# Attention operands of 128 rows in a hybrid decoder trunk: scores from stacked high and low parts, meta values in four groups, a new head order

## The chip, the cores and the metric

The kernel runs on one core of a Trainium2 chip. The metric is the device time of one execution in microseconds (us); of several runs the median is given. One execution was profiled, and all rows below come from it.

## What is computed

The trunk has two layers. The first mixes with a gated linear recurrence, the second with differential attention; a gated MLP with a short causal convolution follows each. 16 learned meta tokens stand ahead of the 512 tokens, so T = 528, D = 1024, 8 heads, and each head has two maps (m = 0, 1) of 64 dimensions. The part that matters here:

```python
def diff_attention(x, w_qkv, lq1, lk1, lq2, lk2, subln_g, w_o, lambda_init):
    q, k, v = jnp.split(x @ w_qkv, 3, axis=-1)     # per head: q, k (2, T, 64), v (T, 128)
    q = apply_rope(q, cos, sin) * (d ** -0.5)
    k = apply_rope(k, cos, sin)
    def attend(q_blk, q_pos):
        s = jnp.einsum('bhmqd,bhmkd->bhmqk', q_blk, k)
        s = jnp.where(mask, s, -jnp.inf)
        p = jax.nn.softmax(s, axis=-1)
        wgt = p[:, :, 0] - lam * p[:, :, 1]
        return jnp.einsum('bhqk,bhkv->bhqv', wgt, v)
    ...                                             # the 16 meta queries, then 4 blocks of 128
    o = rmsnorm(o, subln_g) * (1.0 - lambda_init)
    return o @ w_o
```

## The kernel before

Activations lie with the model dimension on the 128 partitions and tokens along the row. A float32 operand x is used as two rounded parts, hi (a copy of x) and lo = x - hi, so that a product is three matmuls of the fast type: hi hi, lo hi, hi lo (`block_mm`, lines 584 to 595). Weights come as a stream of 128 x 1024 units: SyncE loads a unit (`raw`), ScalarE makes `whi`, VectorE `wlo` (lines 478 to 491). `next_block` asks for units up to seven ahead (line 529).

Nothing is issued in the order of the code. Every operation is a step with an estimated cost for the engines it may run on, and `Program.order` (lines 267 to 348) makes one static order for each engine: it always takes the step that can start first by its estimates, the older one of two, within a window of 180 steps. Buffers of the tag "t" (53 of them) and "half" (5), and the 8 accumulator banks, are given out in that order as well. A step with two possible engines (a copy out of the accumulators) goes to the one that is free first.

In the attention stage `attn_order` (line 96) gives the sequence of the big steps: q, k, v project one head; S makes its scores, A its output, M the meta queries of four heads, W the first half of one tile of the output product. Their steps are interleaved by the planner.

- `rope` (line 1020) projects q or k, rotates it on VectorE (`ra`, `rb`), splits it into a high part (`x[0]`, ScalarE) and `low` (VectorE), and lets SyncE move halves of 64 partitions (`move`, line 1017). Map 0 lies on partitions 0 to 63, map 1 on 64 to 127. For q, `x[m]` gets high and low of map m, one above the other; for k, `x[m]` gets the high part of map m twice, and `low` stays as it is.
- `scores(hd, i)` (line 1061), for query tile i of 128 queries and N = 16 + 128 (i + 1) keys: `score` (line 1069) makes two matmuls for each map. The first is of 128 rows (`k,q` in the rows), the second is of 64 rows, the high q with the low k (`low,q`). For i up to 2 both maps lie in one pair of banks and the order is first, first, second, second; for i = 3 each map has two halves of 264 keys and first and second alternate. Then mask and maximum (VectorE), `e` = exponential (ScalarE), the weights `e` (VectorE: reciprocal, `f`, sum of both maps), transposes of the weights into `tr`, and copies to `wt` (128 real keys a block) and `wm` (the 16 meta keys).
- `values` (line 1050) transposes v in the same way; the 16 meta rows go to `vm`.
- `attend` (line 1108), for each i: one product of the meta keys, 16 rows (`vm,wm`), and i + 1 products of 128 rows (`v,wt`). These are plain float32, and each is two passes (two rows of the profile).
- `meta_queries` (line 1132) does all this for 4 x 4 meta queries at once.

Of the kernel before, what the change touches and what calls it, by code (L numbers as in the profile page):

```python
# [12 lines left out]
F32 = mybir.dt.float32  # L13
# [5 lines left out]
P = 128  # L19
D = 1024  # L20
KD = D // P
SEQ = 512
NMETA = 16
T = SEQ + NMETA
TH = T // 2
OFF1 = 12
# [28 lines left out]
TAIL_TILES = 2  # L55
TBUFS = 53
SBUFS = 30
AHEAD = 180

SPARE = 2  # L60
# [35 lines left out]
def attn_order():  # L96


    order = "q0 k0 q1 S0 k1 v0 q2 A0 k2 S1 k3 k5 v1 q3 S2 k4 S3 v2 q4 A1 v4 A2 v3 S4 k6 A3 q5 q6 A4 S5 k7 v5 S6 q7 v6 S7 A6 M0 v7 W0 A5 W1 W2 W3 W4 W5 M1 W6 A7 W7"
    return [(x[0], int(x[1:])) for x in order.split()]  # L100


# [102 lines left out]
class Program:  # L205
# [61 lines left out]
    def order(self):  # L267
# [9 lines left out]
        while len(out) < len(self.steps):  # L277
# [4 lines left out]
            for e, now in free.items():  # L282
                first = None
                for s in open_steps[e]:
                    if s.rank > oldest + AHEAD:
                        continue
                    start = max(now, s.ready)
                    for b in s.bufs:
                        if b.tag is None or b in held:
                            continue  # L290
                        if b.tag in BANKS:
                            at = self.find_banks(BANKS[b.tag], 0 if s.rank == oldest else s.spare)
                            start = max(start, at[0]) if at else math.inf
                            if not at:
                                break
                            continue
                        if not slots[b.tag]:
                            start = math.inf
                            break
                        start = max(start, slots[b.tag][0])  # L300
                    key = (start, s.rank)
                    if start < math.inf and (first is None or key < first[0]):
                        first = (key, start, s, e)
                if first and (best is None or first[0] < best[0]):
                    best = first
# [53 lines left out]
def trunk_kernel(ctx: ExitStack, tc: tile.TileContext, xT, wstream, wup, par, cst, out):  # L359
# [16 lines left out]
    }  # L376

    def place(tag, bufs):
        places[tag] = lambda b: wp.tile(b.shape, b.dtype, name=b.name, tag=tag, bufs=bufs)

    for tag, n_bufs in w_slots.items():
        place(tag, n_bufs)
# [621 lines left out]
    meta = t_tile("meta", F32, HEADS // MGROUP * GQ + HEADS * NMETA)  # L1004
    qms = [meta[:, g * GQ:(g + 1) * GQ] for g in range(HEADS // MGROUP)]
    km = meta[:, HEADS // MGROUP * GQ:]
    vm = [t_tile(f"vm{i}", F32, 4 * P) for i in range(2)]
    fill(meta, 0.0)
    swap = [(i + 16) % 32 for i in range(32)]
    qk, v_of, sums, wts, wms, o_n = {}, {}, {}, {}, {}, {}  # L1010

    def vmeta(hd):
        return vm[hd // 4].part(hd)[:NMETA, (hd % 4) * P:(hd % 4 + 1) * P]

    ROWS = [slice(64 * m, 64 * m + 64) for m in range(2)]

# [3 lines left out]
    def rope(kind, hd):  # L1020
        segs, n, hn, c0 = (TAIL, T1, TH1, OFF1) if kind == "q" else (FULL, T, TH, 0)
        acc = project(norm.xs, segs, kind)
        a, b = t_tile("ra", F32, n), t_tile("rb", F32, n)
        vec("stream_shuffle", h2(b, 0, hn), acc, swap)
        vec("tensor_tensor", h2(a, 0, hn), acc, h2(cos, c0, hn), op=ALU.mult)
        vec("tensor_tensor", b, b, sin[:, c0:], op=ALU.mult)
        vec("tensor_tensor", a, a, b, op=ALU.add)

        x = [t_tile(f"{kind}{m}", F32R, n) for m in range(2)]
        low = t_tile("low", F32R, n)  # L1030
        top, bottom = ROWS
        act(x[0], a, AF.Copy, n=n)
        vec("tensor_tensor", low, a, x[0].bitcast(F32), n=n, op=ALU.subtract)
        move(x[1].part(1)[bottom], x[0].part(1)[bottom])
        if kind == "q":
            move(x[0].part(1)[bottom], low[top])
            move(x[1].part(0)[top], low[bottom])
        else:
            move(x[1].part(0)[top], x[0].part(1)[bottom])
            move(x[0].part(1)[bottom], x[0].part(0)[top])  # L1040
        qk[kind, hd] = (*x, low)
        if kind == "q":
            for m in range(2):
                g, i = divmod(hd, MGROUP)
                r, col = slice(64 * m, 64 * m + 64), i * 2 * MR + m * MR + i * NQ1
                copy(qms[g].part(("q", hd, m))[r, col:col + NQ1], a[r, :NQ1], n=NQ1, where=("pool",))
        else:
            copy(km.part(("k", hd))[:, hd * NMETA:(hd + 1) * NMETA], a[:, :NMETA], n=NMETA, where=("pool",))

    def values(hd):  # L1050
# [2 lines left out]
        scaled(h2(vt), acc, h2(norm.rstd))  # L1053
        v, tr, trm = t_tile("v", F32, 512), one_tile("tr"), one_tile("tr")
        turn([tr[:, i * P:(i + 1) * P] for i in range(NQT)], [vt[:, NMETA + i * P:NMETA + (i + 1) * P] for i in range(NQT)], ident)
        turn([trm[:NMETA, :P]], [vt[:, :NMETA]], ident)
        copy(v, tr, n=512)
        copy(vmeta(hd), trm[:NMETA, :P], n=P)
        v_of[hd] = v

    def scores(hd, i):
# [5 lines left out]
        S = []  # L1067

        def score(m, o, c0, n):
            return [(o, q[m][:, qs], k[m][:, c0:c0 + n], True, False), (o, q[m].part(m)[ROWS[m], qs], k[2].part(m)[ROWS[m], c0:c0 + n], False, True)]  # L1070

        cost = mm_cost(N)
        if N <= 512:
            s = acc_tile("s")
            (b0, l0), (b1, l1) = (score(m, s[:, m, :N], 0, N) for m in range(2))
            products([b0, b1, l0, l1], 4 * cost, S_SPARE)
            d = s[:, :, N - P:N]
            vec("tensor_tensor", d, d, mask.unsqueeze(1).to_broadcast([P, 2, P]), n=2 * P, op=ALU.add)
            vec("tensor_reduce", mx, s[:, :, :N], n=2 * N, axis=AX.X, op=ALU.max, negate=True)
# [15 lines left out]
        w = es[0]  # L1095
        vec("scalar_tensor_tensor", w, es[1], f, w, n=N, op0=ALU.mult, op1=ALU.add)
        tr, n = one_tile("tr"), (i + 1) * P
        trm = tr[:NMETA, 512 - P:] if n < 512 else one_tile("tr")[:NMETA, :P]
        turn([tr[:, j * P:(j + 1) * P] for j in range(i + 1)], [w[:, NMETA + j * P:NMETA + (j + 1) * P] for j in range(i + 1)], ident)
        turn([trm], [w[:, :NMETA]], ident)  # L1100
        if i == 0:
            wms[hd] = t_tile("wm", F32, 512)
        wt = t_tile("wt", F32, n)
        copy(wt, tr[:, :n], n=n)
        copy(wms[hd].part(i)[:NMETA, i * P:(i + 1) * P], trm, n=P)
        wts[hd, i], sums[hd, i] = wt, rc

    def attend(hd):
# [2 lines left out]
        cols = [slice(i * P, (i + 1) * P) for i in range(NQT)]  # L1111
        for i, c in enumerate(cols):
            oi = o.part(i)[:, c]
            list_ = [(oi, wms[hd].part(i)[:NMETA, c], vmeta(hd), True, False)]
            list_ += [(oi, wts[hd, i][:, cols[j]], v[:, cols[j]], False, j == i) for j in range(i + 1)]
            products(list_, 0.217 * (i + 2), O_SPARE)
        for i, c in enumerate(cols):
            act(junk.part(i)[:, c], o[:, c], AF.Square, n=P, scale=sums[hd, i][:, 0:1], accum_out=ss.part(i)[:, i:i + 1])
        rsqrt_mean(ss, ss, P, NQT)
# [12 lines left out]
    def meta_queries(g):  # L1132
# [10 lines left out]
        act(e, sv, AF.Exp, n=NMETA, bias=mx, accum_out=sm)  # L1143
        vec("reciprocal", sm, sm, n=1)
        vec("tensor_scalar", e, e, sm, coef[:2 * MR], n=NMETA, op0=ALU.mult, op1=ALU.mult)
        tr, w = one_tile("tr"), t_tile("wm", F32, 2 * MR)[:NMETA]
        turn([tr[:NMETA, :2 * MR]], [e], ident[:2 * MR, :2 * MR])
        copy(w, tr[:NMETA, :2 * MR], n=2 * MR, where=("act",))
        vec("tensor_tensor", w[:, :MR], w[:, :MR], w[:, MR:], n=MR, op=ALU.add)
        cols = [slice(i * NQ1, (i + 1) * NQ1) for i in range(MGROUP)]  # L1150
        om_, tot = one_tile("om"), one_tile("tot")
        products([(om_[:, c], vmeta(hd), w[:, c], True, True) for hd, c in zip(hds, cols)], 0.11 * MGROUP)
        om, sq, ro = (t_tile(nm, F32, MR) for nm in ("om", "sq", "ro"))
        copy(om, om_[:, :MR], n=MR, where=("act",))
        act(sq, om, AF.Square, n=MR)
# [156 lines left out]
```

## Time and profile before

| what | value |
|---|---|
| median of 3 runs (lowest to highest) | 1250.38 us (1248.98 to 1251.09) |
| profiled execution, its own time | 1247.84 us |
| its span, first to last instruction | 1245.6 us |
| TensorE busy, share of span | 98% |
| VectorE, ScalarE, GpSimd busy | 79%, 57%, 14% |
| granted clock of TensorE, mean | 0.997 |

PE is TensorE's matmul side, PEld its weight load, DVE is VectorE, ACT ScalarE, POOL GpSimd and SPq SyncE's queue. A matmul's row tells its rows and weight columns, then what is streamed: "64*128 64x264" has 64 rows. Rows of matmuls that follow each other overlap, since they are pipelined; the distance of their starts tells what one costs. The recurrent stage comes first, then the first MLP up to about 570 us, the attention at 575 to 850, and the second MLP behind it.

### The profile page before, as it was taken

The numbers are of one execution on the slowest core, as the hardware profiler recorded it, in microseconds if no ns is written. First come the engines' busy times: TensorE is split into PE (matmuls) and PEld (weight loads), VectorE is DVE, ScalarE is ACT, GpSimd is POOL, SyncE is SP. The second block draws the span as 40 slices with busy tenths as digits, with TensorE's granted clock in tenths as the row PEclk, the third lists the DMA queues.
The fourth block names the chain that finished last, engine by engine and source line by source line (L and its number), as shares of the span: only waits on it lengthen the run. The fifth ranks groups of instructions, "written<-read, shape, count | busy, mean of one in ns | idle before, by whom it ended". The sixth has DMA issues, their size and how long they took to land.

```text
span 1245.6 us, 23369 instructions
## 1 busy us (share of the span) xinstructions
PE 1222.8 (98%) x9288; PEld 1167.6 (94%) x9288; DVE 985.8 (79%) x1562; ACT 714.8 (57%) x1257; POOL 168.4 (14%) x283
## 2 busy tenths in 40 slices
PE   8999999999999999999999999999999999999996
PEld 7999999999999999999988888899999999999985
DVE  6987989977697689779787676668997777778875
ACT  7799565755465466544444444445665555556533
POOL 4000002322222221000000010000222222222100
PEclk9999999999999999999999999999999999999998
DMA  8323425887777877322331233112598777777502
GB/s 302 103 73 102 128 77 128 202 196 184 181 185 175 190 180 195 110 96 73 107 104 54 67 94 136 51 62 91 122 219 202 187 186 186 187 186 183 140 1 68
DMA packets 66350, 171.62 MB, mean 138 GB/s; under 512 B 7872, under 2 KB 10176, under 8 KB 66240
## 3 DMA queue, kind: packets, MB, share of 16 engines
q1 hardware_dynamic: 43200, 128.16, 31.7%
q0 software_dynamic: 23040, 41.95, 20.3%
q8 instruction: 73, 1.20, 0.4%
q14 instruction: 37, 0.30, 0.1%
HBM read 119.63 MB, written 2.10 MB: 98 GB/s over the span
## 4 chain that ended last, share of the span: by engine, by line
PE 82%; DVE 6%; ACT 5%; DMA 3%; issue 2%; POOL 1%; SPq 0%; DVEq 0%; POOLq 0%; ACTq 0%
PE banks L592 45%; PE banks L870 30%; PE banks L463 6%; PE banks L455 2%; ACT L1256 2%; DVE wlo L416 1%; DVE tn L416 1%; ACT r L423 1%; DMA G<-V 1%; ACT whi L485 1%; DVE rc L416 1%; DMA raw<-wstream 1%; ACT tn L423 1%; DMA pt<-par 1%; DMA N<-G 0%
## 5 line engine op out<-in xcount | busy, mean ns | idle before, releaser
L870 PE MATMUL banks<-xh,whi 128*128 128x264 f32 (+1 forms) x960 | 273.3, 285 | 2.3 <-ACT p L431 1.4
L870 PE MATMUL banks<-xl,whi 128*128 128x264 f32 (+1 forms) x960 | 272.6, 284 | 0.0
L870 PE MATMUL banks<-xh,wlo 128*128 128x264 f32 (+1 forms) x960 | 272.1, 283 | 0.0
L592 PE MATMUL banks<-xh,whi 128*128 128x264 f32 (+1 forms) x896 | 188.3, 291 | 8.8 <-ACT whi L423 5.9
L416 DVE TENSOR_TENSOR wlo<-raw,whi 128x1024 fp32r<-128x1024 f32 (+1 forms) x123 | 148.8, 1210 | 59.4 <-ACT whi L485 58.5
L485 ACT CAST whi<-raw 128x1024 fp32r<-128x1024 f32 x121 | 126.2, 1045 | 113.7 <-PE banks L592 46.0
L870 PEld LDWEIGHTS banks<-xh,whi 128*128 128x128 f32 x960 | 181.1, 189 | 6.6 <-ACT p L431 1.9
L870 PEld LDWEIGHTS banks<-xl,whi 128*128 128x128 f32 x960 | 181.2, 189 | 2.2
L592 PE MATMUL banks<-xl,whi 128*128 128x264 f32 (+1 forms) x896 | 182.2, 285 | 0.2 <-DVE xl L416 0.2
L592 PE MATMUL banks<-xh,wlo 128*128 128x264 f32 (+1 forms) x896 | 182.2, 285 | 0.0
L870 PEld LDWEIGHTS banks<-xh,wlo 128*128 128x128 f32 x960 | 181.3, 189 | 0.0
L592 PE MATMUL banks<-actl,whi 128*128 128x264 f32 (+2 forms) x582 | 155.0, 320 | 0.0
L592 PE MATMUL banks<-acth,whi 128*128 128x264 f32 (+2 forms) x582 | 154.9, 320 | 0.0
L592 PE MATMUL banks<-acth,wlo 128*128 128x264 f32 (+2 forms) x582 | 154.6, 319 | 0.0
L592 PEld LDWEIGHTS banks<-xh,whi 128*128 128x128 f32 x896 | 139.1, 190 | 12.3 <-ACT whi L423 5.9
L592 PEld LDWEIGHTS banks<-xl,whi 128*128 128x128 f32 x896 | 139.4, 189 | 0.4 <-DVE xl L416 0.4
L592 PEld LDWEIGHTS banks<-xh,wlo 128*128 128x128 f32 x896 | 139.4, 189 | 0.0
L416 DVE TENSOR_TENSOR h<-banks,h 128x528 f32<-128x528 f32 (+3 forms) x154 | 105.4, 687 | 35.4 <-PE banks L592 34.2
L416 DVE TENSOR_TENSOR wlo<-G,whi 128x512 fp32r<-128x512 f32 (+1 forms) x120 | 103.2, 864 | 23.9 <-ACT whi L577 22.1
L592 PEld LDWEIGHTS banks<-acth,wlo 128*128 128x128 f32 x582 | 96.7, 188 | 8.2
L592 PEld LDWEIGHTS banks<-acth,whi 128*128 128x128 f32 x582 | 96.8, 188 | 6.2
L592 PEld LDWEIGHTS banks<-actl,whi 128*128 128x128 f32 x582 | 96.7, 188 | 6.0
(209 smaller groups left out, 2295.3 us busy)
## 6 DMA issues: line engine op xcount, KB each, us to landing
raw<-wstream SPq DMA_DIRECT2D x105, 512.0 KB, 4.2
G<-wup SPq DMA_DIRECT2D x40, 512.0 KB, 4.0
V<-wup SPq DMA_DIRECT2D x40, 512.0 KB, 3.5
N<-wup SPq DMA_DIRECT2D x40, 256.0 KB, 3.3
G<-V POOLq DMA_DIRECT2D x40, 256.0 KB, 3.6
N<-G POOLq DMA_DIRECT2D x40, 256.0 KB, 4.0
V<-V POOLq DMA_DIRECT2D x40, 256.0 KB, 4.8
G<-N POOLq DMA_DIRECT2D x40, 256.0 KB, 4.4
```

The lines of the kernel that those rows point to most:

```text
L416: step({e: costs[e] for e in where}, lambda e, os_, a, k: getattr(apis[e], fn)(os_[0], *a, **k), [o], args, kw)
L423: nc.scalar.activation(os_[0], a[0], func, **k, **({} if accum_out is None else {"accum_out": os_[1]}))
L455: nc.tensor.transpose(ap(oi), ap(xi), ap(eye))
L463: nc.tensor.matmul(ap(o), ap(l), ap(r), start=start, stop=stop)
L485: prog.add({"act": (n + 118) / 1200}, lambda e: nc.scalar.copy(ap(hi), ap(raw)), [raw], [hi, turn_])
L592: nc.tensor.matmul(a[:, dst, :n], w, m[:, c0:c0 + n], start=s0, stop=s1)
L870: nc.tensor.matmul(a, w[:, c], x, start=start and begin, stop=end, skip_group_check=not start)
L1256: nc.scalar.preload_act_table_set(table)
```

## The change

- k is laid out as high over low (two tiles, no `low` kept), q as high twice and low twice (four tiles). The scores of a map are two matmuls of 128 rows, which give all four products of the parts. First and second of one map stand together. q needs six moves in place of three.
- The 16 meta keys become 64 rows: `meta_parts` writes the high part twice and the low part twice (for v in turns), so that 64 rows of weights times 64 rows of values give all four products. `vm` and `wm` are of the split type, with 64 more rows of zeros that `fill` (GpSimd) writes; the product is one matmul of 128 rows. Each use of `meta_parts` adds a ScalarE copy and a VectorE subtraction of 32 columns ahead of the transpose.
- The meta queries' products of both maps accumulate in the bank, where before the two were added on VectorE.
- `attn_order` has a new sequence; the planner's estimate for `attend` changes. `T_SPARE` is 0, so the changed test for buffers does what it did; the "half" buffers get one common size.

```diff
-    order = "q0 k0 q1 S0 k1 v0 q2 A0 k2 S1 k3 k5 v1 q3 S2 k4 S3 v2 q4 A1 v4 A2 v3 S4 k6 A3 q5 q6 A4 S5 k7 v5 S6 q7 v6 S7 A6 M0 v7 W0 A5 W1 W2 W3 W4 W5 M1 W6 A7 W7"
+    order = "q0 k0 q1 S0 v0 q2 k1 A0 k5 k2 S1 k3 k4 q4 v1 S2 q3 S3 v2 A1 v4 A2 v3 S4 A3 q5 A4 S5 v5 k6 q6 S6 q7 v6 k7 M0 v7 W0 A5 S7 W1 A6 W2 W3 W4 W5 M1 W6 A7 W7"
...
-    vm = [t_tile(f"vm{i}", F32, 4 * P) for i in range(2)]
+    vm = [t_tile(f"vm{i}", F32R, 4 * P) for i in range(2)]
+    for x in vm:
+        fill(x[MSEG:].bitcast(F32), 0.0)
...
+    def meta_parts(name, x, rows=P, turns_=False):
+        o = Buf("half", [rows, MSEG], F32R, name)
+        o4 = o.rearrange("p (a b c) -> p a b c", a=2, b=2)
+        hi, lo = (o4[:, :, i] if turns_ else o4[:, i] for i in range(2))
+        x = x.unsqueeze(1).to_broadcast([rows, 2, NMETA])
+        act(hi, x, AF.Copy, n=2 * NMETA)
+        vec("tensor_tensor", lo, x, hi.bitcast(F32), n=2 * NMETA, op=ALU.subtract)
+        return o.bitcast(F32)
...
-        if kind == "q":
+        if kind == "k":
             move(x[0].part(1)[bottom], low[top])
             move(x[1].part(0)[top], low[bottom])
+            qk[kind, hd] = x
         else:
-            move(x[1].part(0)[top], x[0].part(1)[bottom])
-            move(x[0].part(1)[bottom], x[0].part(0)[top])
-        qk[kind, hd] = (*x, low)
+            low1 = t_tile("low", F32R, n)
+            move(low1.part(1)[bottom], low.part(1)[bottom])
+            for y0, y1 in (x, (low, low1)):
+                move(y1.part(0)[top], y0.part(1)[bottom])
+                move(y0.part(1)[bottom], y0.part(0)[top])
+            qk[kind, hd] = (*x, low, low1)
...
-        turn([trm[:NMETA, :P]], [vt[:, :NMETA]], ident)
+        turn([trm[:MSEG, :P]], [meta_parts("vs", vt[:, :NMETA], turns_=True)], ident)
...
-            return [(o, q[m][:, qs], k[m][:, c0:c0 + n], True, False), (o, q[m].part(m)[ROWS[m], qs], k[2].part(m)[ROWS[m], c0:c0 + n], False, True)]
+            return [(o, q[i][:, qs], k[m][:, c0:c0 + n], i < 2, i >= 2) for i in (m, 2 + m)]
...
-            (b0, l0), (b1, l1) = (score(m, s[:, m, :N], 0, N) for m in range(2))
-            products([b0, b1, l0, l1], 4 * cost, S_SPARE)
+            products(score(0, s[:, 0, :N], 0, N) + score(1, s[:, 1, :N], 0, N), 4 * cost, S_SPARE)
...
-        turn([trm], [w[:, :NMETA]], ident)
+        turn([trm], [meta_parts("ws", w[:, :NMETA])], ident)
...
-            list_ = [(oi, wms[hd].part(i)[:NMETA, c], vmeta(hd), True, False)]
+            list_ = [(oi, wms[hd].part(i)[:, c], vmeta(hd), True, False)]
...
-            products(list_, 0.217 * (i + 2), O_SPARE)
+            products(list_, 0.12 + 0.22 * (i + 1), O_SPARE)
...
-        products([(om_[:, c], vmeta(hd), w[:, c], True, True) for hd, c in zip(hds, cols)], 0.11 * MGROUP)
+        products([(om_[:, c], vmeta(hd), w[:, m * MR + c.start:m * MR + c.stop], m == 0, m == 1) for hd, c in zip(hds, cols) for m in range(2)], 0.22 * MGROUP)
```

How this moves instructions is shown at three places. In these lists `ident` is the unit matrix of a transpose, `e` the weights of a query tile, `ws` the four groups of its meta keys; numbers behind a name tell tiles apart.

TensorE, head 0, the scores of i = 2 and the first product of `attend` behind them. Before:

```order
L455 MATMUL banks<-ident,e 128x128
L455 MATMUL banks<-ident,e 16x128
L592 MATMUL banks<-xh,whi 128x258 x2
L592 MATMUL banks<-xl,whi 128x258 x2
L592 MATMUL banks<-xh,wlo 128x258 x2
L463 MATMUL banks<-k_7139,q_7107 128x400
L463 MATMUL banks<-k_7149,q_7119 128x400
L463 MATMUL banks<-low,q_7107 128x400
L463 MATMUL banks<-low,q_7119 128x400
L463 MATMUL banks<-vm_7325,wm 128x128
L463 MATMUL banks<-v,wt 128x128
```

Now:

```order
L458 MATMUL banks<-ident,ws 64x128
L595 MATMUL banks<-xh,whi 128x264 x2
L595 MATMUL banks<-xl,whi 128x264 x2
L595 MATMUL banks<-xh,wlo 128x264 x2
L466 MATMUL banks<-k_7146,q_7111 128x400
L466 MATMUL banks<-k_7146,low 128x400
L466 MATMUL banks<-k_7156,q_7123 128x400
L466 MATMUL banks<-k_7156,low 128x400
L466 MATMUL banks<-vm_6438,wm 128x128
L466 MATMUL banks<-v,wt 128x128
```

First and second product of a map now follow each other, `low` is q's and not k's, and the transpose of the meta part no longer stands straight behind that of the real keys: here projection blocks lie between them.

VectorE, head 0, around the weights `e` of i = 0. Before:

```order
L416 RECIPROCAL rc<-sm 128x2
L416 TENSOR_TENSOR banks<-banks,mask 128x2x128
L416 SCALAR_TENSOR_TENSOR f<-rc,sm,nlam 128x1
L431 COPY vm_7325<-banks 16x128
L416 TENSOR_REDUCE mx<-banks 128x2
L416 SCALAR_TENSOR_TENSOR e<-e,f 128x144
L416 RECIPROCAL rc<-sm 128x2
L431 COPY wm<-banks 16x128
```

Now:

```order
L419 RECIPROCAL rc<-sm 128x2
L419 TENSOR_TENSOR banks<-banks,mask 128x2x128
L419 SCALAR_TENSOR_TENSOR f<-rc,sm,nlam 128x1
L419 TENSOR_TENSOR ra<-ra,rb 128x516
L419 SCALAR_TENSOR_TENSOR e<-e,f 128x144
L419 TENSOR_REDUCE mx<-banks 128x2
L419 TENSOR_TENSOR low<-ra,q_7343 128x516
L419 TENSOR_TENSOR ws<-e,ws 128x32
```

The subtraction for `ws` is new; here it stands two instructions behind `e`.

SyncE, from the end of a run of weight loads to the moves of head 0's q and k. Before:

```order
L480 DMA raw<-wstream 128x1024 x16
L446 DMA q_7119<-q_7107 64x516
L446 DMA q_7119<-low 64x516
L446 DMA k_7149<-k_7139 64x528 x2
L446 DMA q_7107<-low 64x516
```

Now:

```order
L483 DMA raw<-wstream 128x1024 x15
L449 DMA q_7123<-q_7111 64x516 x2
L449 DMA low<-low 64x516 x2
L449 DMA k_7156<-k_7146 64x528
L449 DMA q_7111<-q_7111 64x516
L449 DMA k_7156<-low 64x528
L449 DMA low<-low 64x516
L483 DMA raw<-wstream 128x1024
L449 DMA k_7146<-low 64x528
```

q's moves are six in place of three, and a weight load now stands among them.

## Rows read from the trace of the kernel before

**Rows 1.** The page, its first part: busy us, share of the span, instructions.

```profile
PE 1222.8 (98%) x9288; PEld 1167.6 (94%) x9288; DVE 985.8 (79%) x1562; ACT 714.8 (57%) x1257; POOL 168.4 (14%) x283
```

**Rows 2.** Busy time by stretch: length, each engine's us, granted clock, DMA share, GB/s.

```profile
580.00:770.00 190.00, 190.00 (x1407) 171.10 (x1405) 148.30 (x315) 87.51 (x240) 7.94 (x23) 1.00 0.32 93
50.00:250.00 200.00, 197.85 (x1601) 195.53 (x1600) 174.49 (x244) 151.19 (x212) 18.80 (x42) 1.00 0.44 118
200.00:250.00 50.00, 48.76 (x388) 47.48 (x388) 47.39 (x74) 34.45 (x61) 15.37 (x25) 1.00 0.82 181
```

**Rows 3.** Groups by shape, 570 to 852 us: count, busy us, mean ns, idle before.

```profile
L463 PE MATMUL banks<-vm,wm 16*128 16x128 f32 x64 | 15.5, 321 | 0.0
...
L463 PE MATMUL banks<-low,q 64*128 64x264 f32 x32 | 12.3, 385 | 0.0
```

**Rows 4.** Timeline of TensorE, a last-tile score: start us, us, what.

```profile
688.93 0.37 PE L463 MATMUL banks<-k,q 128*128 128x264 f32 x1
689.23 0.39 PE L463 MATMUL banks<-low,q 64*128 64x264 f32 x1
689.54 0.39 PE L463 MATMUL banks<-k,q 128*128 128x264 f32 x1
689.86 0.39 PE L463 MATMUL banks<-low,q 64*128 64x264 f32 x1
690.18 0.51 PE L592 MATMUL banks<-xh,whi 128*128 128x264 f32 x2
690.52 0.41 PE L592 MATMUL banks<-xl,whi 128*128 128x264 f32 x2
690.77 0.41 PE L592 MATMUL banks<-xh,wlo 128*128 128x264 f32 x2
```

**Rows 5.** Timeline of TensorE, a score of the first tile.

```profile
699.84 0.34 PE L463 MATMUL banks<-k,q 128*128 128x144 f32 x2
700.11 0.34 PE L463 MATMUL banks<-low,q 64*128 64x144 f32 x2
700.38 0.51 PE L592 MATMUL banks<-xh,whi 128*128 128x264 f32 x2
700.73 0.41 PE L592 MATMUL banks<-xl,whi 128*128 128x264 f32 x2
```

**Rows 6.** Timeline of TensorE, a part of `attend` and the score behind it.

```profile
706.04 0.48 PE L463 MATMUL banks<-vm,wm 16*128 16x128 f32 x2
706.45 0.71 PE L463 MATMUL banks<-v,wt 128*128 128x128 f32 x4
707.10 0.48 PE L463 MATMUL banks<-vm,wm 16*128 16x128 f32 x2
707.51 0.94 PE L463 MATMUL banks<-v,wt 128*128 128x128 f32 x6
708.20 0.61 PE L463 MATMUL banks<-k,q 128*128 128x400 f32 x2
```

**Rows 7.** Timeline of TensorE, behind the last head's output transposes.

```profile
828.87 0.50 PE L592 MATMUL banks<-oh,whi 128*128 128x258 f32 x2
829.66 0.51 PE L592 MATMUL banks<-ol,whi 128*128 128x258 f32 x2 [0.28 <-DVE ol L416]
```

**Rows 8.** Groups by shape, 575 to 835 us, short ones of ScalarE and VectorE.

```profile
L423 ACT ACTIVATE sq<-om 128x16 f32<-128x16 f32 x2 | 0.4, 218 | 0.1
L416 DVE TENSOR_TENSOR om<-om,ro 128x16 f32<-128x16 f32 x2 | 0.3, 168 | 0.0
```

**Rows 9.** The moves' line, 575 to 835 us: ns min, median, max; time to landing.

```profile
L446 SPq DMA_DIRECT2D q<-low x16: 461/462/548, 581.2 to 761.5; - x16
...
DMA to landing us min/median/max: 2.2/2.2/4.3
```

**Rows 10.** Timeline, the weights `e` of a tile and their transposes.

```profile
714.99 0.63 DVE L416 SCALAR_TENSOR_TENSOR e<-e,f 128x400 f32<-128x400 f32 x1
...
715.91 0.60 PE L455 MATMUL banks<-ident,e 128*128 128x128 f32 x4
```

More of the change, by code (lines that the diff above doesn't have):

```diff
@@ L23 @@
 NMETA = 16
+MSEG = 4 * NMETA
 T = SEQ + NMETA
@@ L57 @@
 SBUFS = 30
+NEAR, T_SPARE = 20, 0
 AHEAD = 180
@@ L296, in order @@
                             continue
-                        if not slots[b.tag]:
+                        if len(slots[b.tag]) <= (T_SPARE if b.tag == "t" and s.rank > oldest + NEAR else 0):
                             start = math.inf
@@ L378, in place @@
     def place(tag, bufs):
-        places[tag] = lambda b: wp.tile(b.shape, b.dtype, name=b.name, tag=tag, bufs=bufs)
+        padded = {"padded_shape": [P, TH]} if tag == "half" else {}
+        places[tag] = lambda b: wp.tile(b.shape, b.dtype, name=b.name, tag=tag, bufs=bufs, **padded)
     for tag, n_bufs in w_slots.items():
@@ L1012, in vmeta @@
     def vmeta(hd):
-        return vm[hd // 4].part(hd)[:NMETA, (hd % 4) * P:(hd % 4 + 1) * P]
+        return vm[hd // 4].part(hd)[:, (hd % 4) * P:(hd % 4 + 1) * P]
+    def meta_parts(name, x, rows=P, turns_=False):
[6 more added lines that the diff above has]
+        return o.bitcast(F32)
     ROWS = [slice(64 * m, 64 * m + 64) for m in range(2)]
@@ L1055, in values @@
         turn([tr[:, i * P:(i + 1) * P] for i in range(NQT)], [vt[:, NMETA + i * P:NMETA + (i + 1) * P] for i in range(NQT)], ident)
-        turn([trm[:NMETA, :P]], [vt[:, :NMETA]], ident)
+        turn([trm[:MSEG, :P]], [meta_parts("vs", vt[:, :NMETA], turns_=True)], ident)
         copy(v, tr, n=512)
-        copy(vmeta(hd), trm[:NMETA, :P], n=P)
+        copy(vmeta(hd)[:MSEG], trm[:MSEG, :P], n=P)
         v_of[hd] = v
@@ L1097, in scores @@
         tr, n = one_tile("tr"), (i + 1) * P
-        trm = tr[:NMETA, 512 - P:] if n < 512 else one_tile("tr")[:NMETA, :P]
+        trm = tr[:MSEG, 512 - P:] if n < 512 else one_tile("tr")[:MSEG, :P]
         turn([tr[:, j * P:(j + 1) * P] for j in range(i + 1)], [w[:, NMETA + j * P:NMETA + (j + 1) * P] for j in range(i + 1)], ident)
-        turn([trm], [w[:, :NMETA]], ident)
+        turn([trm], [meta_parts("ws", w[:, :NMETA])], ident)
         if i == 0:
-            wms[hd] = t_tile("wm", F32, 512)
+            wms[hd] = t_tile("wm", F32R, 512)
+            fill(wms[hd][MSEG:].bitcast(F32), 0.0)
         wt = t_tile("wt", F32, n)
         copy(wt, tr[:, :n], n=n)
-        copy(wms[hd].part(i)[:NMETA, i * P:(i + 1) * P], trm, n=P)
+        copy(wms[hd].part(i)[:MSEG, i * P:(i + 1) * P], trm, n=P)
         wts[hd, i], sums[hd, i] = wt, rc
@@ L1145, in meta_queries @@
         vec("tensor_scalar", e, e, sm, coef[:2 * MR], n=NMETA, op0=ALU.mult, op1=ALU.mult)
[L1146 to L1149, printed above, removed]
+        tr, w = one_tile("tr"), t_tile("wm", F32R, 2 * MR)
+        turn([tr[:MSEG, :2 * MR]], [meta_parts("es", e, 2 * MR)], ident[:2 * MR, :2 * MR])
+        fill(w[MSEG:].bitcast(F32), 0.0)
+        copy(w[:MSEG], tr[:MSEG, :2 * MR], n=2 * MR, where=("act",))
         cols = [slice(i * NQ1, (i + 1) * NQ1) for i in range(MGROUP)]
         om_, tot = one_tile("om"), one_tile("tot")
-        products([(om_[:, c], vmeta(hd), w[:, c], True, True) for hd, c in zip(hds, cols)], 0.11 * MGROUP)
+        products([(om_[:, c], vmeta(hd), w[:, m * MR + c.start:m * MR + c.stop], m == 0, m == 1) for hd, c in zip(hds, cols) for m in range(2)], 0.22 * MGROUP)
         om, sq, ro = (t_tile(nm, F32, MR) for nm in ("om", "sq", "ro"))
```

## The prediction

> **What bounds the kernel now.** I read the shares of the engines first, then the busy time by stretch, then the attention stage instruction by instruction. TensorE is busy for 98% of the span, VectorE for 79% and ScalarE for 57% [rows 1]. The attention stage lies at about 575 to 850 us. From 580 to 770, its dense part, TensorE shows no idle time at all, at the full granted clock (1.00, the 2.4 GHz level), while VectorE has 148.3 of 190 us and ScalarE 87.5 [rows 2]. So this stage lasts as long as TensorE's instructions follow each other, and what one of them costs is the distance from its start to the next start, not the length of its row (the rows overlap). TensorE's only waits that the groups below show are at the very end [rows 7].
>
> **What a matmul of fewer rows costs.** In the projections a pair of 128-row matmuls over 264 columns starts 0.25 us after the pair ahead (690.52 to 690.77), 0.123 each [rows 4]. In a score of the last query tile (`i` = 3) 128-row and 64-row matmuls alternate: k, low, k, low and the next projection's pair take 688.93 to 690.52, 1.59 us for six matmuls [rows 4]. At 0.123 each they would take 0.74. Every change of the row count, in either direction, thus costs about 0.2 us: 0.85 over the five starts. In `attend`, a 16-row pair `vm,wm` takes 0.41 us (706.04 to 706.45), four `v,wt` with a 16-row pair behind take 0.65, and six with a 128-row matmul behind take 0.69 [rows 6]. The six give 0.115 each, so the four contain 0.19 of waiting for the switch. That last step also goes from fp32 operands to the split ones and to another weight tile without a gap; so it is neither the type nor the new weights that costs, but the rows.
>
> **The change part by part, on TensorE.**
> - Scores, `i` = 3: all four matmuls get 128 rows. There are two such places per head, 16 in all (the 32 rows of 264 columns, [rows 3]): 16 x 0.85 = 13.6 us less.
> - Scores, `i` = 0 to 2: 24 places, one switch in and one out, but the two 64-row matmuls stand side by side and run together. For 144 columns the four and the projection pair behind take 699.84 to 700.73, 0.89 us [rows 5]. Afterwards there are four 128-row ones: two of them take 0.27 now [rows 5], so 0.54 + 0.25 = 0.79; at the 0.115 of `v,wt` [rows 6], 0.46 + 0.25 = 0.71. That is 0.10 to 0.18 less. I have no row here for 272 and 400 columns; between 0 and 0.3 less, I take 0.2 for all 24: 4.8 us less (2.4 to 7).
> - Attend: 32 products of 16 rows, two passes each (64 rows, [rows 3]). Each costs 0.41 + 0.19 = 0.60 us now. Afterwards it is one 128-row matmul of 128 columns in one pass, by the nearest row 0.115 (0.135 by the score's): 32 x 0.485 = 15.5 us less (14.9 to 15.5).
> - Six of the 16-row products stand straight behind a 64-row one in the order of before, and I have counted that switch twice: 6 x 0.19 = 1.1 back.
> - The transposes of meta columns have 64 columns of weights in place of 16 and remain one instruction each; the meta queries have as many matmuls as before and lose a few switches. I set both at 0.
>
> Sum on TensorE: 13.6 + 4.8 + 15.5 - 1.1 = 32.8, rounded to **33 us less (30 to 35)**.
>
> **What the others get.** 42 small pieces (32 of weights, 8 of values, 2 of meta queries) add one ScalarE copy and one VectorE subtraction each, of 32 columns. The nearest rows, of 16 columns, are 218 and 168 ns [rows 8]: 9.2 us on ScalarE and 7.1 us on VectorE, less two small additions that go. Both lie beside TensorE's work as long as those engines have room. In 580 to 770 VectorE would have 148.3 plus about 5.5 in a stretch that is 190/250 of 33 = 25 us shorter: 154 of 165, 93%. GpSimd gets 12 fills of zeros, ahead of use, on an engine that is busy for 8 of 190 us [rows 2]. SyncE gets 24 more half-tile moves, since q now needs six and k still three: 24 x 0.46 = 11 us of issuing, 2.2 us each to land [rows 9]. Each q has two that wait for the landing of others, and weight loads queue behind them; weights are asked for up to seven units ahead (line 529), and DMA has a share of 0.32 there [rows 2], so I set this at 0 (0 to 2).
>
> **New waits.** TensorE becomes the shorter one, so I ask what is late next. The recurrent stage and the first MLP tiles behind it run projections of the same kind without switches: at 50 to 250 us VectorE has 87% and TensorE stands still 2.15 of 200 us, 1.1%; at 200 to 250, with 95%, 1.24 of 50, 2.5% [rows 2]. The attention would be some 217 us with 93% in its dense part: 2.4 to 5.4 us, I take 3.2. Second, the meta weights' transpose now comes two engines later than the others of its tile: `e`, copy, subtraction, transpose. At the tightest place that I found `e` is ready at 715.62 and its transpose starts at 715.91 [rows 10]: 0.29 us to spare, while copy and subtraction take 0.39 and two hand-overs. In the new order most of these transposes stand one or more projection blocks (0.74 us) behind, but ten of the 32 have less than 0.6 us of other work ahead. 10 x 0.13 = 1.3 (0 to 6). Third, at the end of the stage the last head's `ol` is late: from 828.87 to 829.66 TensorE starts one pair where 0.25 would do, 0.54 lost [rows 7]. In the new order four blocks of other heads stand there: 0.5 less. Sum of waits: 3.2 + 1.3 - 0.5 = 4 us.
>
> So 33 - 4 = 29 us less. The profiled execution of before took 1247.84 (span 1245.6), so the same execution would take 1218.8. The median of the runs is 2.5 above the profiled one: 1221.3, **forecast 1221 us**.
>
> **Rivals.**
> - A, nothing becomes late: 1250.4 - 33 - 0.5 = 1217, down to 1215 with the upper bound of 35. For it: in 580 to 770 TensorE stood still nowhere, though the same chains ran beside it [rows 2]; against: the stretch of 50 to 250 lost 1.1%, its last quarter 2.5%.
> - B, VectorE becomes the bound of the dense part, since waits between engines keep it from more than the 87% of 50 to 250: 154 / 0.87 = 177 in place of 165. That costs 12 rather than the 3.2 above: 1230. Against it stand the 95% at 200 to 250.
> - C, slower: the chain scores, mask, maximum, exponential, `e`, copy, subtraction, transpose takes the place of the switches. Place: the 32 `ws` transposes; in the order of VectorE a subtraction can stand behind a maximum and a `low` of 0.7 us. It decides when each of the 32 makes TensorE stand over 1.0 us on average (33/32). At 1.15, 1250.4 - 33 + 36.8 = 1254.
> - D, slower: the gaps are not the row count's. Then they stay, and the change only takes away that the two 64-row matmuls of `i` = 0 to 2 run together: in rows 5 two 64-row ones take the 0.27 us of two others with a switch inside them. 24 x 0.14 = 3.4 more, with 1.3 of waits 1255. Against it: the step from `v,wt` to `k,q` without a gap [rows 6]. The Trainium skill (TensorE: Matmul & The Clock Gate, Part 3) speaks against this change: matmuls on different row groups run concurrently, so 128-row operands give a pairing up. The Trainium skill (TensorEngine Tiling (Array Packing), Key Properties) has the other side too: changing the tiling mode drains the engine. The trace shows both, the pairing in rows 5 and the switches in rows 4 and 6, and the switches are the dearer.
>
> **How the numbers follow.** Forecast 0.64, A 0.12, B 0.18, C 0.03, D 0.03. The range goes from A's lower end, 1215, to just above B, 1231; outside lie C, D and the edges of A and B, under 0.2. Under 0.2% (2.5 us) a measurement of this kernel can't be told from no change; the forecast, A and B are all beyond it. Faster 0.94, same 0.01, slower 0.05.
>
> **What would show it.** Right: in the changed trace a last-tile score and the projection pair behind it take about 0.75 us from start to start where 1.59 stood, and the `vm,wm` row comes once per product with 128 rows and about 0.12 to its successor; the stage ends about 29 us earlier, and nothing else moves. VectorE's share in the dense part is near 93%. Wrong: TensorE idle of over 8 us in the stage, ended by VectorE at `e`, `ws` or `low` (B, C), or moves of q ending TensorE's waits at the first score of a head; or 128-row matmuls that still start 0.3 us apart (D).

## The result and the profile after

The changed kernel takes 1217.86 us (median of 4 runs, 1217.1 to 1219.96), the kernel before beside it 1249.72 (4 runs): a ratio of 0.9748, 95% interval 0.9733 to 0.9762, so 31.9 us less. The forecast was 1221, 1215 to 1231. The profiled execution of after took 1218.53, against 1218.8 by the sum for the profiled execution. The 2.5 us that I had added for the median lie in the spread between executions: the profiled one of before was quicker than all four beside which after was timed.

The page of after, its first part, with the columns of [rows 1]:

```profile
PE 1192.3 (98%) x9256; PEld 1160.7 (95%) x9256; DVE 984.8 (81%) x1598; ACT 722.2 (59%) x1303; POOL 172.3 (14%) x295
```

TensorE is still what the span consists of. As marks of the attention stage I use the first sums of squares of the two MLPs (rows `ssh,ones_r`): 568.93 to 854.85 before, 285.9 us; 570.03 to 827.85 after, 257.8 us. So the stage gave 28.1 of the profiled executions' 29.3 us. What lies ahead of it took 1.1 us more, what lies behind it 1.8 us less.

Timeline of TensorE in after, with the columns of [rows 4]: a score of the first tile, one of the last tile, the products of `attend` for `i` = 3, and the first score of head 0 at its wait:

```profile
593.26 0.34 PE L466 MATMUL banks<-k,q 128*128 128x144 f32 x1 [1.22 <-DMA k<-low]
...
623.87 0.23 PE L466 MATMUL banks<-k,q 128*128 128x144 f32 x1
...
624.28 0.62 PE L458 MATMUL banks<-ident,os 128*128 128x128 f32 x4
...
636.03 0.28 PE L466 MATMUL banks<-k,q 128*128 128x264 f32 x1
636.15 0.28 PE L466 MATMUL banks<-k,low 128*128 128x264 f32 x1
636.27 0.28 PE L466 MATMUL banks<-k,q 128*128 128x264 f32 x1
636.39 0.28 PE L466 MATMUL banks<-k,low 128*128 128x264 f32 x1
636.51 0.41 PE L595 MATMUL banks<-xh,whi 128*128 128x258 f32 x2
636.76 0.40 PE L595 MATMUL banks<-xl,whi 128*128 128x258 f32 x2
...
663.51 0.22 PE L466 MATMUL banks<-vm,wm 128*128 128x128 f32 x1
663.57 1.11 PE L466 MATMUL banks<-v,wt 128*128 128x128 f32 x8
664.43 0.49 PE L595 MATMUL banks<-xh,whi 128*128 128x264 f32 x2
```

The last tile's four and the pair behind them take 636.03 to 636.76, 0.73 us, where [rows 4] has 1.59: four starts exactly 0.12 apart. The first tile's four take 0.41 (623.87 to 624.28), and with 0.25 for a projection pair that is 0.66, where [rows 5] has 0.89. In `attend` the meta product and the eight passes of `v,wt` take 0.92 together, 0.102 each; nothing is left of the 0.60 that a 16-row pair cost by [rows 6]. Counted over the whole stage, successive matmuls of TensorE change their row count 176 times in before and 4 times in after.

The busy time by stretch in after, columns of [rows 2]; its dense part is now 580 to 745:

```profile
580.00:770.00 190.00, 188.03 (x1550) 186.31 (x1550) 162.81 (x392) 107.84 (x334) 10.18 (x34) 0.99 0.42 121
...
580.00:745.00 165.00, 163.75 (x1361) 163.01 (x1361) 141.90 (x332) 92.11 (x269) 9.25 (x30) 1.00 0.43 117
```

TensorE is idle for 1.25 us in the dense part. VectorE has 141.9 of 165, 86%. All waits of TensorE at 575 to 800 us in after (us in total, times, longest):

```profile
PE banks L466 <- DMA k<-low: 1.2, 1, 1.2
PE banks L466 <- ACT wt L434: 0.4, 1, 0.4
PE banks L466 <- ACT sq L426: 0.3, 1, 0.3
```

The first is at the very first score, 593.26. The other two are at the meta queries of heads 0 to 3, at 759.01 and 759.91. What follows them doesn't stand among the waits: busy time in stretches of 2 us, the granted clock third from the end:

```profile
758.00:760.00 2.00, 1.29 (x9) 0.83 (x8) 1.57 (x6) 1.97 (x12) 0.00 (x0) 1.00 0.99 395
760.00:762.00 2.00, 2.00 (x12) 2.00 (x13) 1.39 (x8) 2.00 (x9) 0.09 (x1) 0.64 0.54 215
762.00:764.00 2.00, 2.00 (x11) 2.00 (x11) 1.61 (x6) 0.78 (x4) 0.00 (x0) 0.51 0.00 0
764.00:766.00 2.00, 2.00 (x20) 2.00 (x19) 2.00 (x5) 1.56 (x6) 0.00 (x0) 1.00 0.00 0
```

TensorE was busy for 1.29 of 2 us, and from about 760.5 to 764.0 it ran at 0.5, the 1.2 GHz level: 11 matmuls in 2 us, 20 in the next 2. Those 3.4 us cost half of that, 1.7 us, though the engine counts as busy all the time.

### The profile page after: what moved, and what is told of

It reads as the page before. It is cut to its first block, busy times and chain, and to the rows that moved or that the text cites. A ratio compares the mean times of both kernels' runs of the same rounds, so it can differ in the third digit from the quotient of the medians.

```text
span 1216.8 us, 23450 instructions
## 1 busy us (share of the span) xinstructions
PE 1192.3 (98%) x9256; PEld 1160.7 (95%) x9256; DVE 984.8 (81%) x1598; ACT 722.2 (59%) x1303; POOL 172.3 (14%) x295
## 4 chain that ended last, share of the span: by engine, by line
PE 82%; ACT 5%; DVE 5%; DMA 3%; issue 2%; POOL 1%; SPq 0%; DVEq 0%; POOLq 0%; ACTq 0%
PE banks L595 46%; PE banks L873 31%; PE banks L466 4%; ACT L1276 2%; PE banks L458 2%; DVE wlo L419 1%; DVE tn L419 1%; ACT r L426 1%; ACT whi L488 1%; DMA raw<-wstream 1%; DVE rc L419 1%; DMA N<-G 1%; DMA pt<-par 1%; ACT tn L426 1%; DMA k<-low 0%
## 6 DMA issues: line engine op xcount, KB each, us to landing
N<-wup SPq DMA_DIRECT2D x40, 256.0 KB, 3.3
G<-V POOLq DMA_DIRECT2D x40, 256.0 KB, 3.7
N<-G POOLq DMA_DIRECT2D x40, 256.0 KB, 4.0
V<-V POOLq DMA_DIRECT2D x40, 256.0 KB, 4.9
G<-N POOLq DMA_DIRECT2D x40, 256.0 KB, 4.7
```

## The experiments

The stage in the table is the distance between the same two marks in the profiled execution; times are medians of 4 to 6 runs. The last column is the part of that stage that TensorE spent at the granted clock 0.5 (1.2 GHz) in this execution; half of it is lost time. "Before" and "after" name the kernel that was edited.

| label | edit | median us | before beside | ratio, 95% | stage us | at 0.5 |
|---|---|---|---|---|---|---|
| (before) | | 1249.72 | | | 285.9 | 0 |
| (after) | | 1217.86 | 1249.72 | 0.9733 to 0.9762 | 257.8 | 3.4 |
| e_more_switches | before, scores of i < 3 alternate | 1261.68 | 1249.36 | 1.0086 to 1.0116 | 297.9 | 0 |
| h_fewer_switches | before, scores of i = 3 grouped | 1243.12 | 1249.36 | 0.9935 to 0.9968 | 279.6 | 0 |
| f_rows_alone | before, meta product of 128 rows, type kept | 1237.93 | 1249.36 | 0.9893 to 0.9923 | 274.8 | 0 |
| a_order_alone | before, new head order | 1253.84 | 1249.49 | 1.0022 to 1.0045 | 290.4 | 10.2 |
| c_scores_alone | a, and the new scores | 1235.79 | 1249.49 | 0.9872 to 0.9905 | 274.3 | 6.8 |
| d_meta_alone | a, and the new meta groups | 1238.69 | 1249.49 | 0.9895 to 0.9925 | 274.9 | 3.4 |
| b_old_order | after, old head order | 1227.80 | 1249.49 | 0.9811 to 0.9840 | 264.6 | 6.8 |
| k_no_split_old_order | b, no groups of meta keys | 1224.45 | 1249.38 | 0.9788 to 0.9815 | 263.4 | 3.4 |
| l_subtract_twice | after, new subtractions doubled | 1219.61 | 1249.38 | 0.9745 to 0.9772 | 256.3 | 0 |
| g_meta_early | after, v0 and M0 earlier | 1219.40 | 1249.36 | 0.9746 to 0.9775 | 256.0 | 0 |
| i_v0_first | after, v0 earlier | 1221.34 | 1249.38 | 0.9764 to 0.9791 | 259.0 | 0 |
| j_m0_early | after, M0 earlier | 1219.21 | 1249.38 | 0.9746 to 0.9773 | 255.8 | 0 |

**Is it the switch of rows? More of them and fewer.** Both keep every matmul of the kernel before and only exchange neighbours.

```diff
-            products([b0, b1, l0, l1], 4 * cost, S_SPARE)
+            products([b0, l0, b1, l1], 4 * cost, S_SPARE)
```

> The kernel before, with the four score matmuls of query tiles 0 to 2 in alternating order (first, second, first, second in place of first, first, second, second). Nothing else moves; the instructions and the planner's order are the same. Theory (each change of the row count costs TensorE about 0.2 us, and TensorE sets the time of the attention stage): 24 places get two more changes and lose the pairing of the 64-row matmuls, 24 x (0.38 + 0 to 0.14) = 9 to 12.5 us slower, 1259 to 1262. Rival D (the gaps belong to something else than the row count): only the pairing is lost, 3.4 us slower, 1253. If another engine set the time: no change, 1250.

```diff
-                products(score(m, s[:, 0, :hn], 0, hn) + score(m, s[:, 1, :hn], hn, hn), 2 * cost, S_SPARE)
+                (b0, l0), (b1, l1) = score(m, s[:, 0, :hn], 0, hn), score(m, s[:, 1, :hn], hn, hn)
+                products([b0, b1, l0, l1], 2 * cost, S_SPARE)
```

> The kernel before, with the four score matmuls of a map in the last query tile grouped (two of 128 rows, then two of 64) in place of alternating. Theory: 16 places lose two changes of the row count each, 16 x 2 x 0.19 = 6 us faster, 1244; both 64-row matmuls lie on the same rows, so they do not pair. Rival D: no change, 1250. If another engine set the time: no change.

The first is 12.3 us slower, the second 6.2 us faster. Timelines of TensorE, the first tile of e_more_switches and the last tile of h_fewer_switches:

```profile
706.17 0.23 PE L463 MATMUL banks<-k,q 128*128 128x144 f32 x1
706.33 0.33 PE L463 MATMUL banks<-low,q 64*128 64x144 f32 x1
706.59 0.33 PE L463 MATMUL banks<-k,q 128*128 128x144 f32 x1
706.85 0.33 PE L463 MATMUL banks<-low,q 64*128 64x144 f32 x1
707.11 0.51 PE L592 MATMUL banks<-xh,whi 128*128 128x264 f32 x2
707.46 0.40 PE L592 MATMUL banks<-xl,whi 128*128 128x264 f32 x2
```

```profile
686.52 0.49 PE L463 MATMUL banks<-k,q 128*128 128x264 f32 x2
686.94 0.51 PE L463 MATMUL banks<-low,q 64*128 64x264 f32 x2
687.38 0.51 PE L592 MATMUL banks<-xh,whi 128*128 128x264 f32 x2
687.72 0.41 PE L592 MATMUL banks<-xl,whi 128*128 128x264 f32 x2
```

Alternating makes 1.29 us of the 0.89 of [rows 5]; grouping makes 1.20 of the 1.59 of [rows 4], two changes fewer at 0.39 us. For 272 and 400 columns alternating makes 1.53 of 1.02 and 1.80 of 1.23 (means of the places with a projection pair behind). Against four 128-row matmuls and the pair in after (0.66, 0.75 and 0.98) the four changes cost 0.63, 0.78 and 0.82: 0.16 each for 144 columns and about 0.2 for the longer ones. The 0.09 to 0.16 that alternating adds beyond two such changes is what the two 64-row matmuls side by side had saved. So a change costs 0.16 to 0.2 us, and it can be had back by order alone. Rival D (the gaps aren't the rows') is out; so is the gain in full: grouping by itself brings 6 of the 13.6.

**Is it the rows or the type, in `attend`?** The meta product gets 128 rows, 112 of them zeros, and stays plain float32 in two passes.

```diff
+    for x in vm:
+        fill(x, 0.0)
...
+            fill(wms[hd], 0.0)
...
-            list_ = [(oi, wms[hd].part(i)[:NMETA, c], vmeta(hd), True, False)]
+            list_ = [(oi, wms[hd].part(i)[:, c], vmeta(hd), True, False)]
```

> The kernel before, with the meta product of attend on 128 rows (16 of values, 112 of zeros), still plain float32 in two passes; no split, no new copies or subtractions, scores and head order as before. Theory: each of the 32 products costs two passes of 0.115 = 0.23 in place of 0.60, 32 x 0.37 = 12 us faster, 1238. Rival D (the type, plain float32 beside the split type, makes the gaps): no change, 1250. The difference to the change's own 15.5 is the second pass, 32 x 0.115 = 3.7 us.

11.4 us faster. Timeline of TensorE in f_rows_alone:

```profile
702.19 0.39 PE L463 MATMUL banks<-vm,wm 128*128 128x128 f32 x2
702.42 0.39 PE L463 MATMUL banks<-v,wt 128*128 128x128 f32 x2
702.64 0.39 PE L463 MATMUL banks<-vm,wm 128*128 128x128 f32 x2
702.86 0.61 PE L463 MATMUL banks<-v,wt 128*128 128x128 f32 x4
```

A `vm,wm` pair takes 0.22 to 0.23 where it took 0.60: zeros in 112 rows cost less than leaving them out. What the four groups and the split type add to that is the second pass, by the rows of after 0.1 us a product.

**What is each part worth?** The head order alone, each operand change on top of it, and the whole change without the order.

```diff
-    order = "q0 k0 q1 S0 k1 v0 q2 A0 k2 S1 k3 k5 v1 q3 S2 k4 ..."
+    order = "q0 k0 q1 S0 v0 q2 k1 A0 k5 k2 S1 k3 k4 q4 v1 S2 q3 ..."
```

> The kernel before with the new sequence of the big steps alone. Theory: TensorE has the same instructions and had next to no waits in the stage, so nothing is to be gained: within 2 us of 1250; the end of the stage may give 0.5 to 0.8. Rival (the sequence itself is worth a good part of the 32 us): 10 us faster or more.

c_scores_alone adds the new tiles of q and k and their moves to that, with this score:

```diff
-            return [(o, q[m][:, qs], k[m][:, c0:c0 + n], True, False), (o, q[m].part(m)[ROWS[m], qs], k[2].part(m)[ROWS[m], c0:c0 + n], False, True)]
+            return [(o, q[i][:, qs], k[m][:, c0:c0 + n], i < 2, i >= 2) for i in (m, 2 + m)]
```

> The kernel before with the scores' new operands and the new sequence, the meta product as before (16 rows). Theory: 13.6 + 4.8 = 18.4 us less, up to 1.1 of the switches shared with a 16-row product back, waits 0 to 2: 1232 to 1234. Rival C (new waits take the place): less than 12 us.

d_meta_alone is after with the same lines taken back, and b_old_order is after with the first diff's `order` taken back.

> The changed kernel with the scores' operands as before: only the meta product in four groups and the new sequence. Theory: 15.5 us less, up to 1.1 shared back, waits of the new small pieces 0 to 2: 1235 to 1237. Rival C (the chain through the new copy and subtraction makes TensorE wait): less than 10 us.

> The changed kernel with the old sequence of the big steps. Theory: the switches are gone all the same; some more waits of TensorE, since the sequence was made for another balance: 1218 to 1224. Rival B (VectorE bounds the dense part, and the new sequence is what spreads its work): over 1226.

Three of the four expectations missed by about 2 us, and that for b_old_order by 4. The order alone isn't free: +4.35 us, which the prediction had not costed, and with it c and d lie above what I expected. In a_order_alone a wait of 0.51 us for `sq` of the meta queries ends at 784.10, and from 785.3 to 795.6 TensorE runs at the lower clock:

```profile
786.00:796.00 10.00, 10.00 (x40) 8.45 (x40) 5.31 (x17) 3.71 (x14) 0.09 (x1) 0.50 0.40 151
```

Half of those 10.2 us, 5.1, is more than the 4.5 by which its stage is longer than that of before; so in this execution the lower clock is the whole price of the order. Its other executions agree: the mean granted clock of all six is 0.989 to 0.992, where before beside them has 0.996 to 0.997.

With a_order_alone as the ground, the scores bring 18.05 us by the medians and the meta groups 15.15, where the sum of before had 18.4 and 15.5. That nearness is in part luck: by the table c has 3.4 us less at the lower clock than its ground and d 6.8 less, so 1.7 and 3.4 us of these gains are clock, and d has 1.8 us more in single stops than a (a stop is what the distance between two starts has beyond the usual one, where that is over 0.4 us). Both together bring 36.0 from that ground, 2.8 more than the 33.2 that the parts add up to; what makes up the rest I haven't followed. e, h and f, without any lower clock, are the better measure of the price.

Yet with the new operands the same order is worth 9.9 us: b_old_order takes that much more than after, and lies where I had put rival B. In it TensorE has ten single stops of 9.8 us together (by distances of starts), and 6.8 us at the lower clock behind the meta queries (751.6 to 758.4). Two of the stops are waits for a new subtraction: 1.44 us for `es` of the meta queries (749.47) and 0.93 for a `ws`. The second, in the timeline of VectorE and TensorE of b_old_order:

```profile
649.05 1.22 DVE L419 TENSOR_TENSOR wlo<-raw,whi 128x1024 fp32r<-128x1024 f32 x1
...
650.18 0.18 DVE L419 TENSOR_TENSOR ws<-e,ws 128x32 fp32r<-128x32 f32 x1
...
650.42 0.30 PE L458 MATMUL banks<-ident,ws 128*64 128x128 f32 x1 [0.93 <-DVE ws L419]
```

The subtraction stands behind a `wlo` of 1.22 us, and the transpose waits for it. That is rival C's mechanism, at one of the 32 `ws` transposes. The load of VectorE (rival B) isn't it: at 580 to 770 it is busy for 157.4 of 190 us there, 83%, less than in after over the same stretch (162.8).

**Is the price of the small pieces hidden?** k_no_split_old_order is b_old_order with the meta product of f_rows_alone, so without any small piece (`meta_parts` is out, `list_` as in the diff of f_rows_alone); l_subtract_twice issues each new subtraction twice in its step, and every engine's order stays as in after.

```diff
+        def twice(e, os_, a, k):
+            for _ in range(2):
+                nc.vector.tensor_tensor(os_[0], *a, **k)
...
-        vec("tensor_tensor", lo, x, hi.bitcast(F32), n=2 * NMETA, op=ALU.subtract)
+        step({"dve": (2 * NMETA + 62) / 960}, twice, [lo], (x, hi.bitcast(F32)), {"op": ALU.subtract})
```

> The changed kernel with every new VectorE subtraction of the small pieces done twice, within the same step, so that the order of every engine stays the same: 42 x 0.18 = 7.6 us more on VectorE, 6 of it in the dense part. Theory (TensorE is still the bound, VectorE has 13% of room there): 0 to 2 us slower than the changed kernel, 1218 to 1220. Rival B (VectorE bounds the dense part): 5 to 7 us slower, 1223 to 1225. Rival C (the chain through these pieces is what TensorE waits for): each of the 32 transposes 0.1 to 0.18 later, 3 to 6 us slower.

> The changed kernel with the old sequence and the meta product in plain float32 on 128 rows (two passes, no split, none of the 42 small pieces); to be held against b_old_order, 1227.8, which has the small pieces and 9.8 us in single waits of over 0.4 us. If those waits come from the small pieces' chain or load (rivals B, C, for that sequence): 1222 to 1225, although the second pass costs 3.7 us. If they come from the sequence itself: 3.7 us slower than it, 1230 to 1232.

Doubling them costs 1.75 us by the medians, where rivals B and C would have cost 3 us or more, and the intervals of l_subtract_twice and after overlap. Busy time by stretch, and the subtractions' group:

```profile
580.00:770.00 190.00, 188.56 (x1561) 186.10 (x1560) 170.29 (x435) 108.77 (x336) 10.50 (x35) 1.00 0.43 121
```

```profile
L1031 DVE TENSOR_TENSOR ws<-e,ws 128x32 fp32r<-128x32 f32 x64 | 11.9, 188 | 2.6 <-ACT ws L426 1.5
```

VectorE goes from 86% to 90% and TensorE keeps its 188 of 190: VectorE isn't the bound (rival B). In the old order it is another matter: k_no_split_old_order has 3.7 us more of matmul passes than b_old_order and is 3.35 us faster, so by the medians the pieces cost about 7 us there. Its single stops come to 5.8 us, b's to 9.8, and its time at the lower clock is 3.4 us, b's 6.8: 4.0 and half of 3.4, 5.7 us by the profiled executions. The planner also makes another order without the pieces, so this is their price with the order that it made for them. It suggests that what the new order buys is mostly room for the pieces; the new order without them was not run.

l_subtract_twice shows one thing more. With the orders of after, its profiled execution has waits for the same two things at the meta queries (0.29 and 0.24 us; TensorE busy for 1.67 of 2 us at 758 to 760, 1.76 at 760 to 762), but the clock stays at 1.00 throughout 758 to 766, the wait at the first score is 0.5 in place of 1.2, and its stage is 1.6 us shorter than after's. So neither the 1.7 us of lower clock nor the full length of the first wait comes with the program in each execution.

**Can the two rests be had?** v0 ahead of S0 gives the first head's moves more time; M0 ahead of A4 puts the meta queries where more other work lies around them. g_meta_early does both, i_v0_first the first and j_m0_early the second.

```diff
-    order = "q0 k0 q1 S0 v0 q2 ... q5 A4 S5 ... k7 M0 v7 ..."
+    order = "q0 k0 q1 v0 S0 q2 ... q5 M0 A4 S5 ... k7 v7 ..."
```

> The changed kernel with another sequence of the big steps: v0 ahead of S0, and M0 earlier (behind q5) so that W0 does not wait for its chain. Theory (what is lost in the changed kernel's attention stage are two single waits, 1.5 us at the first head's scores for the moves of k, and 1.1 us at the meta queries with the half clock behind it, 1.7 us): 2 to 4 us faster than the changed kernel, 1214 to 1216. Rival B (VectorE is the bound of the dense part): the waits come back elsewhere, 1217 to 1219.

> The changed kernel with v0 ahead of S0 in the sequence, nothing else. Theory: TensorE's wait of 1.5 us for the landing of k's last half at the first scores (593 us) goes, since a projection of 5.9 us stands ahead of it: 1.5 us faster, 1216.4. Rival: the sequence makes as large a wait elsewhere: 1217 to 1219.

> The changed kernel with M0 behind q5 in place of behind k7, nothing else. Theory: the two waits at the meta queries (759 to 760 us, 1.1 us) go and with them the 3.4 us at the half clock behind, which cost 1.7: up to 2.8 us faster, 1215 to 1217. Rival: waits of the same size come up elsewhere, as they did when both moves were made together: 1217 to 1220.

None beats after, though I had expected it of each: by the medians they are 1.5, 3.5 and 1.35 us slower; for g and j the intervals overlap with after's. j_m0_early shows where it goes. Its stage is 2.0 us shorter, without a stretch at the lower clock, and what lies behind, up to the end of the last matmul, takes 382.6 in place of 379.9. (Its profiled execution also reached the stage 1.65 us later than after's, which belongs to no edit that I know of.) Its waits at 885 to 915 us, in the second MLP:

```profile
ACT nhi L488 <- DMA N<-G: 3.6, 1, 3.6
...
PE banks L873 <- ACT z L434: 1.7, 3, 0.8
```

There a chain of DMAs and GpSimd steps (`N`, `G`, `V`) ends in `nhi` on ScalarE, and `z`, for which TensorE waits, stands behind it. After has none of these waits on PE. That the moved work makes this chain late is only argued: no run changed the chain. In i_v0_first the wait at 593 is gone, but the planner gave new places to steps all along the stage, and some 5 us of other stops, by distances of starts, came up at 720 to 778.

## Why the prediction came out right, point by point

- **What a change of rows costs** (0.85 per last-tile score, 0.2 per other score, 0.485 per meta product): right. e, h and f confirm the price by order or zeros alone: 48 changes more, 32 fewer and 56 fewer, for +12.3, -6.2 and -11.4 us, or 0.195 a change for h and 0.2 for f. Inside the sum two errors offset each other. [rows 4] shows one of the dearer places: over all that have a projection pair behind, a last-tile score and the pair take 1.52 in the mean before and 0.75 after, so 0.77 and not 0.85, 12.3 us and not 13.6. The other scores gave 0.2 to 0.25, about 5.6 us and not 4.8. The 1.1 for switches counted twice was taken from the order; the trace of before has these six places, but their price was not tested by itself.
- **The sum.** The stage shrank by 28.1 us. After has 4.2 us of loss by distances of starts (1.4 at 593, 0.55 twice at 759 to 760, 1.7 of clock), and before lost about 0.8 at its end [rows 7]. So 28.1 + 4.2 - 0.8 = 31.5 went on TensorE, against 33 (30 to 35).
- **New waits, 4 us: wrong in kind, and right in size by luck.** The 3.2 us by analogy with the recurrent stage's 1.1% didn't come as many small stops: the dense part from 595 to 745 has none that the profile shows. In their place stand two spots, both of which I had set at 0. One is the term of SyncE's moves (0 to 2): it was 1.4, at the first score of head 0, and close to what I had named as a sign of being wrong, though the move is k's and not q's. The queue of SyncE in after, at the first head:

```profile
586.61 0.58 SPq L483 DMA_DIRECT2D raw<-wstream  x1
587.28 0.46 SPq L449 DMA_DIRECT2D k<-low  x1
587.79 1.23 SPq L449 DMA_DIRECT2D q<-q  x2
589.07 2.79 SPq L449 DMA_DIRECT2D low<-low  x2
```

The move at 587.28 lies straight behind a weight load of 512 KB. The slowest landing at 580 to 600 took 5.9 us, which for this move would be 593.2, and the score that waits for `k<-low` starts at 593.26. The landing's median over the stage is 2.3 us. That the load ahead delays it was not shown; it is only its place. In l_subtract_twice the same load stands as far ahead of the same move (586.90 and 587.57), and the score starts 5.3 us behind the move, where it was 6.0 here. The other spot is the meta queries: their chain of short steps made TensorE stop twice, and in after's profiled execution the lower clock followed.
- **The `ws` transposes, 1.3 (0 to 6):** none of TensorE's waits in after is for `ws`, and by distances of starts the latest of the 32 transposes loses 0.25 us; the nearest is a wait of 0.4 in l_subtract_twice. So the ten tight places that I counted had room. In the old order the small pieces cost 5.7 to 7 us, at or above the top of what I had allowed for the new one.
- **The end of the stage, -0.5:** the `ol` wait is gone, and about 0.8 with it, since the pair ahead of it in [rows 7] had started late too.
- **VectorE, 93%:** wrong, 86%. The new pieces are there, at 184 ns for a subtraction where I took 168. But VectorE's total fell from 985.8 to 984.8 us while ScalarE's rose by 7.4: among others, copies to `wt` that may run on either went to ScalarE (VectorE has 12 before, 8 after). And of the 12 us that were missing from 154, 6.4 lie behind the stretch: VectorE has 61.6 us at 745 to 828 in after, where it had 55.2 at 770 to 855 before. I had assumed that the shorter stretch would hold the same work.
- **Head order:** the prediction gave it only the order's tight places and the stage's end. It is a term of its own, of either sign: +4.35 with the old operands, by way of the lower clock, and -9.9 with the new ones.
- **Rivals.** The median, 1217.9, lies nearer to A's 1217 than to the forecast. But A's reason, that nothing becomes late, isn't what happened: about 4 us were lost to stops and the lower clock. It was the step from the profiled execution to the median that failed: +2.5 us before, -0.7 after. B falls with l, D with e, h and f, C with after's waits, though b shows its mechanism at work.

The Trainium skill (TensorE: Matmul & The Clock Gate, Part 3) let a pairing on row groups speak against the change. The pairing is real: it saved 0.09 to 0.16 us a place by e. But the two changes around it cost 0.3 to 0.4, more than it saves. The Trainium skill (TensorEngine Tiling (Array Packing), Key Properties) says that a change of mode drains the engine; the trace agrees that a change of rows costs time, 0.16 to 0.2 us here, and no run here shows that it is a drain.

Left open: in which executions the lower clock comes, and why the medians are 31.9 apart where the two profiled executions are 29.3 apart. Of these 2.6 us, 1.1 lie ahead of the stage, where after's profiled execution was slower.

## What to carry to other kernels

Where matmuls of full and of fewer rows take turns, read the distance of starts around each turn: here a change in row count cost about 0.2 us in either direction, more than the matmul itself, so group equal ones first (6 us for two lines), and fill up with zeros before anything cleverer (11 us). A new small step on a chain is cheap only with work of others around it: in one head order doubling the new subtractions cost nothing that could be told, in another the pieces cost 6 to 7 us, so choose the order anew with the operands, not before. When parts are measured one by one, look at the granted clock of each ground: here it was worth up to 5 us between two orders of the same work. And look behind the stage too: the run that won 2.0 us in the stage lost 2.7 behind it.

## What the hardware did that I had not expected

- Two short stops, 1.29 of 2 us busy, were followed by 3.4 us at a granted clock of 0.5 (1.2 GHz) in after. In a_order_alone one stop, 1.59 of 2 us busy, was followed by 10.2 us; in b_old_order the stops at 746 to 750, 1.76 of 4 us busy, by 6.8. TensorE counts as fully busy there, so neither the waits nor its share show it, only the granted clock and the halved count of matmuls do (40 in 10 us in a_order_alone). With the same order of steps on each engine and stops of 1.67 and 1.76 of 2 us busy, l_subtract_twice stayed at 1.00; what decides between them no run here told apart.
- The row-count change costs about the same in the two kinds that this kernel has: 0.19 us between 128 and 16 rows with plain float32 (f_rows_alone), 0.195 between 128 and 64 with the split type at 264 columns (h_fewer_switches).
- 64 columns of weights in place of 16 in the transposes (272 ns a row, `ident,ws`, 32 in after) last as long as the 128-column ones beside them (273, `ident,e`).
